# Four conditioning tiles on GpSimd, RMS chains placed anew, and a down product finished tile by tile

## The chip, the cores and the metric

The kernel runs on one core of a Trainium2 chip. The metric is the device time of one execution in microseconds (us). The engines are TensorE (PE; its weight loads are PEld), VectorE (DVE), ScalarE (ACT), GpSimd (POOL) and SyncE (SP, which here only issues DMAs). Each runs its instructions in order and waits on semaphores.

## The reference

One layer (DEPTH = 1) on 1024 tokens of width 1024: a Fourier mixer and a gated ConvFFN, each with an RMS norm in front and a gate behind, and a last RMS norm.

```python
m = jax.nn.silu(c) @ w_mod + b_mod                 # sh1, sc1, gt1, sh2, sc2, gt2
a = rms_norm(x, g_mix) * (1 + sc1) + sh1
f = jnp.fft.fft2(a.reshape(1, L, 4, 256), axes=(1, 3), norm="ortho").real
h = x + gt1 * (f.reshape(1, L, D) @ w_fnet_out)
a2 = rms_norm(h, g_ffn) * (1 + sc2) + sh2
g, v = jnp.split(a2 @ w_up, 2, axis=-1)            # 2 x 2816 columns
g = depthwise_conv3(g) + b_conv
h = h + gt2 * ((jax.nn.silu(g) * v) @ w_down)
return rms_norm(h, g_final)
```

## The kernel before

Activations lie transposed: 8 tiles (`dt`) of 128 features, with even tokens in columns 0 to 511 (block 0) and odd ones in 512 to 1023 (block 1). Most products run as three passes on operands split in a rounded high part ("h") and a remainder ("l").

**Conditioning.** The vector `m` has 6 sections. A section `s` is 8 tiles of `w_mod` (128x1024, `wm`), each multiplied with silu(c) and summed along its rows by one VectorE instruction (`mod_sum`, L145), with silu(c) in PSUM (`silp`). The tiles come over 7 buffers; SP loads tile k+7 when tile k has been used. Section 2 is the mixer's gate, 4 and 3 are scale and shift of the second norm.

**Step 2 of the Fourier transform** (L411 to L446) makes, for each of 4 groups `g`, three PSUM tiles `s2p`, `s2p`, `s2q`, from six banks that are used in turn. `split` (L402 ScalarE, L403 VectorE) turns them into `ph`, `pl`, `qh`, `ql`; `p1` (L421, L422) does it for one extra row. The functions `between[g]` put `w_lo` (L366, remainder of the output weights), `w_last` (L381, L382) and conditioning tiles between the groups on VectorE. GpSimd makes sums and differences of weights first (`w_prep`, L357, L358).

**`fnet_block`** (L533, L536) multiplies with the output weights: per block 8 tiles `dt`, 25 matmuls each (13 into `pw`, 12 into `qw`). ScalarE (L550, L551) and VectorE (L542) write the result to `ha`, GpSimd issues a DMA that adds `x` to it (L555); then ScalarE squares it (L471) and VectorE or GpSimd adds that to `sacc` (L476). `while_even` and `while_odd` run after each `dt`, `amid_odd` inside it.

**The RMS chain** of a block: `rstd_col` sums `sacc` over partitions on TensorE (`ssps`, L485), VectorE scales (L487), GpSimd takes the power -1/2 (L489); `rstd_diag` (L494) makes diagonals, and `rstd_row` broadcasts them by a matmul (`rb`, L499). `norm2` (L572, L573, L567) then makes the FFN's operands `a2`.

**FFN.** `plain` and `product` (L693) make the first three chunks of the up product, each from `op_hi` (L612) and `op_lo` (L616); the other 19 go through a Strassen-like scheme (X, Y, Z). The down product has 7 products of 11 steps into PSUM banks `dX`, `dY`; a step is 12 matmuls, three for each of four tiles `g` (L1091). Its end is the last norm of the odd half: add (L697), square (L1133), sum (`cols`, L1065), power, diagonal, broadcast, `last_norm` (L697), store (L1078).

Up to step 2 the order on PE, ACT and POOL is a scheduler's and that on DVE and SP the code's; from `fnet_block(0)` ACT and POOL follow the code too, and from `fnet_block(1)` PE does.

Of the kernel before, what the change touches and what calls it, by code (L numbers as in the profile page):

```python
# [30 lines left out]
KT = 8  # L31
# [13 lines left out]
def fourier_ffn_kernel(ctx: ExitStack, tc: tile.TileContext, xf, xs, xt, cb, wmod, vecs, cst, ml, sp, wfa, wfb, wfl, wup,  # L45
# [346 lines left out]
    mod_tiles(4, 0, 4)  # L392
# [35 lines left out]
    def gate_ffn():  # L428
# [90 lines left out]
    def fnet_block(blk, then, mid=lambda dt: None):  # L519
# [5 lines left out]
        for dt in range(KT):  # L525
# [3 lines left out]
            for ps, s, ah, al, m, c0 in ((pw, 1, ph, pl, n, pc), (qw, 0, qh, ql, 256, qc)):  # L529
# [51 lines left out]
    def while_even(dt):  # L581
# [11 lines left out]

    fnet_block(0, while_even)
# [41 lines left out]

    def while_odd(dt):
        if dt > 2:

            squares(1, dt - 3)  # L640
            spill(1, dt - 3)
            stat(1, dt - 3)
        if dt == 0:
# [4 lines left out]
        elif 1 < dt < 6:
            norm2(0, even[1], {2: (1, 2), 3: (3, 4), 4: (5, 6), 5: (7,)}[dt])
            if dt == 3:  # L650
                for n in ("A11", "A12", "A21", "A22"):
                    ops[0, n] = op_hi(part(0, n), f"op0{n}")
        if dt > 5:
            for n in (("A11", "A12"), ("A21", "A22"))[dt - 6]:
                op_lo(ops[0, n], part(0, n))

    def amid_odd(dt):

        if dt == 1:
            even.append(rstd_col(sacc[0], 512))  # L660
            tb.append(stage("tb"))
            rstd_diag(even[0], 512, tb[0][:, 512:])
        elif dt == 2:
            even.append(rstd_row(512, tb[0][:, 512:]))
# [4 lines left out]
    fnet_block(1, while_odd, amid_odd)  # L669
# [151 lines left out]
    for dt in (5, 6, 7):  # L821
        squares(1, dt)
        spill(1, dt)
        stat(1, dt)
# [28 lines left out]
    op_lo(ops[1, "A11"], part(1, "A11"))  # L853
    op_lo(ops[1, "A12"], part(1, "A12"))
# [205 lines left out]
    def cols(tiles):  # L1060

        ps = small("ssps")
        for n, t in enumerate(tiles):
            for j in range(4):
                nc.tensor.matmul(ps[:, j:j + 1], lhsT=t[:, j * P:(j + 1) * P], rhs=ones[:, 0:1],  # L1065
                                 start=(n == 0 and j == 0), stop=(n == len(tiles) - 1 and j == 3))
# [157 lines left out]
```

## Time and profile before

| | us |
|---|---|
| three runs: median (lowest to highest) | 825.66 (824.72 to 827.84) |
| the profiled execution's own time | 826.69 |
| its span, first to last instruction | 824.9 |
| PE busy | 778.9 |
| DVE busy | 606.7 |
| ACT busy | 344.4 |
| POOL busy | 128.2 |
| mean granted TensorE clock | 0.977 of full speed |

A busy share is a mean over stages with different limits, so it says little here. The tables by stretch show when TensorE waited and at which clock it ran; the waits say for whom.

### The profile page before, as it was taken

The page shows a single profiled execution, that of the slowest core. Times are in us where ns is not written, and L with a number is a line of the kernel's source. Part 1 is how long each engine was busy: PE and PEld are TensorE (multiplying, and loading weights), DVE is VectorE, ACT ScalarE, POOL GpSimd, SP SyncE. Part 2 cuts the span into 40 slices and gives each one's busy share as a digit, 9 for nine tenths or more (in the row PEclk, how much of TensorE's full clock was granted, in tenths as well). Part 3 has the DMA queues.
Part 4 walks back from the last instruction along what each step waited for, and adds up shares of the span by engine and source line. Part 5 has one row for each costly group of instructions (what it writes and reads, how often), then busy time and mean ns, then how long its engine had stood idle before and what let it go on. Part 6 is the DMA issues. An engine that isn't in the chain of part 4 may idle for free.

```text
span 824.9 us, 10510 instructions
## 1 busy us (share of the span) xinstructions
PE 778.9 (94%) x3588; PEld 633.3 (77%) x3588; DVE 606.7 (74%) x1001; ACT 344.4 (42%) x617; POOL 128.2 (16%) x168
## 2 busy tenths in 40 slices
PE   1998979799999999999999999999999999999994
PEld 0585978588888888888888888888888888888883
DVE  5998976697867777877777777776747766648573
ACT  7364425425623334343333334433544435345520
POOL 2053431100112121212121121212110000000000
PEclk9999989799999999999999999999999999999995
DMA  9999764702398777858597778676999765655532
GB/s 331 407 335 341 217 178 91 217 27 89 89 288 204 199 192 205 242 142 246 146 254 198 193 221 256 141 195 155 266 294 356 231 191 184 199 183 176 182 149 102
DMA packets 81959, 171.30 MB, mean 208 GB/s; under 512 B 9001, under 2 KB 13865, under 8 KB 81906
## 3 DMA queue, kind: packets, MB, share of 16 engines
q1 hardware_dynamic: 67218, 143.89, 49.6%
q0 software_dynamic: 14688, 26.75, 20.4%
q8 instruction: 28, 0.46, 0.2%
q14 instruction: 25, 0.20, 0.1%
HBM read 130.49 MB, written 51.64 MB: 221 GB/s over the span
## 4 chain that ended last, share of the span: by engine, by line
PE 82%; DVE 9%; DMA 3%; issue 2%; ACT 2%; POOL 1%; POOLq 0%; DVEq 0%; SPq 0%; ACTq 0%
PE Y L693 19%; PE dX L1091 15%; PE X L693 13%; PE Z L693 13%; PE dY L1091 11%; PE c L693 8%; DVE wm L145 2%; DMA ha<-in_xt 2%; DMA wm<-in_wmod 1%; DVE ha L542 1%; PE ssps L1065 1%; DVE ha L572 1%; DVE z L216 1%; PE s2p L441 1%; DVE w L216 1%
## 5 line engine op out<-in xcount | busy, mean ns | idle before, releaser
L616 DVE TENSOR_TENSOR dn<-wd,dn 128x512 fp32r<-128x512 f32 x154 | 99.9, 689 | 69.3 <-ACT dn L612 68.6
L612 ACT CAST dn<-wd 128x512 fp32r<-128x512 f32 x154 | 88.6, 618 | 99.8 <-PE dX L1091 41.5
L1091 PE MATMUL dX<-dn,dn 128*128 128x512 f32 x528 | 123.5, 394 | 0.0
L1091 PEld LDWEIGHTS dX<-dn,dn 128*128 128x128 f32 x528 | 99.1, 188 | 23.2 <-issue 0.5
L755 POOL DMA_DIRECT2D ha<-ha x44 | 38.9, 968 | 348.2 <-DVE ha L696 158.7
L1091 PE MATMUL dY<-dn,dn 128*128 128x512 f32 x396 | 92.1, 394 | 0.0
L1091 PEld LDWEIGHTS dY<-dn,dn 128*128 128x128 f32 x396 | 74.4, 188 | 17.2
L696 DVE TENSOR_TENSOR ha<-Y,ha 128x512 f32<-128x512 f32 x57 | 39.4, 690 | 25.6 <-PE Y L693 25.6
L979 ACT COPY ha<-X 128x512 f32<-128x512 f32 x19 | 11.1, 586 | 110.2 <-PE X L693 110.2
L742 ACT ACTIVATE ha<-ha 128x512 f32<-128x512 f32 x44 | 27.8, 632 | 57.2 <-DVE ha L697 57.2
L145 DVE CUSTOM_DVE_ANT_0 wm<-wm,silp 128x1024 f32<-128x1024 f32 x32 | 37.9, 1213 | 0.4 <-DMA wm<-in_wmod 0.2
L1069 POOL TENSOR_TENSOR r<-r,mhalf 128x4 f32<-128x4 f32 x2 | 2.0, 1020 | 200.6 <-DVE r L1068 200.6
L798 POOL DMA_DIRECT2D sg_s<-in_wdn x22 | 29.9, 1373 | 9.2 <-DMA sg_s<-in_wdn 9.2
L798 POOL DMA_DIRECT2D sg_s<-sg_s x22 | 27.5, 1258 | 16.8 <-DMA sg_s<-sg_s 9.8
L697 DVE SCALAR_TENSOR_TENSOR ha<-ha,vec 128x512 f32<-128x512 f32 (+1 forms) x38 | 28.6, 752 | 1.4
L697 DVE SCALAR_TENSOR_TENSOR ha<-X,vec,ha 128x512 f32<-128x512 f32 (+1 forms) x38 | 28.4, 746 | 0.7
L696 DVE TENSOR_TENSOR ha<-Z,ha 128x512 f32<-128x512 f32 x38 | 26.0, 685 | 1.2 <-PE Z L693 1.2
L166 PE MATMUL gr<-wm,sil 128*32 128x512 f32 x32 | 10.3, 771 | 15.2 <-ACT sil L256 15.1
L696 DVE TENSOR_TENSOR ha<-ha 128x512 f32<-128x512 f32 x33 | 22.4, 685 | 0.0
L771 ACT COPY ha<-ha 128x512 f32<-128x512 f32 x11 | 6.8, 621 | 33.7 <-DVE ha L697 33.7
L166 PEld LDWEIGHTS gr<-wm,sil 128*32 128x32 f32 x32 | 3.1, 131 | 23.0 <-issue 20.6
L555 POOL DMA_DIRECT2D ha<-in_xt x14 | 12.7, 927 | 43.4 <-DVE ha L542 37.5
(947 smaller groups left out, 2000.2 us busy)
## 6 DMA issues: line engine op xcount, KB each, us to landing
wm<-in_wmod SPq DMA_DIRECT2D x40, 512.0 KB, 7.5
ha<-ha POOLq DMA_DIRECT2D x44, 256.0 KB, 5.2
sg_s<-in_wdn SPq DMA_DIRECT2D x44, 256.0 KB, 6.0
wd<-sg_s SPq DMA_DIRECT2D x44, 256.0 KB, 2.7
us_u<-ha SPq DMA_DIRECT2D x33, 256.0 KB, 2.0
wd<-in_wdn SPq DMA_DIRECT2D x33, 256.0 KB, 3.1
wd<-us_u SPq DMA_DIRECT2D x33, 256.0 KB, 3.4
us_T<-ha SPq DMA_DIRECT2D x22, 256.0 KB, 5.2
```

The costliest lines, as they stand in the source:

```text
L145: nc.vector.tensor_tensor_reduce(out=t, in0=t, in1=silp, scale=1.0, scalar=0.0, op0=ALU.mult, op1=ALU.add, accum_out=mods[:, s, n:n + 1])
L166: nc.tensor.matmul(rows[x][32 * j:32 * j + 32, :], lhsT=sil32[:, 4 * q + j, :], rhs=tiles[j][:, 512 * x:512 * x + 512], start=(q == 0), st ...
L216: nc.vector.scalar_tensor_tensor(out=t, in0=xraw[4 * i + f + 1][:, cs_], scalar=rr[:, 4 * i + f + 1:4 * i + f + 2], in1=xraw[4 * i + f][:, ...
L612: nc.scalar.copy(out=t[:, HALF[0]], in_=src)
L616: eng.tensor_tensor(out=t[:, HALF[1]], in0=src, in1=t[:, HALF[0]].bitcast(F32), op=ALU.subtract)
L693: nc.tensor.matmul(ps, lhsT=lh, rhs=rh, start=(first and j == 0 and x == 0), stop=(last and j == 3 and x == 2), skip_group_check=more)
L696: tt = lambda out, a, b, op, eng=nc.vector: eng.tensor_tensor(out=out, in0=a, in1=b, op=op)
L697: stt = lambda out, a, s, b, op0, op1: nc.vector.scalar_tensor_tensor(out=out, in0=a, scalar=s, in1=b, op0=op0, op1=op1)
L742: nc.scalar.activation(out=u[c, blk], in_=u[c, blk], func=AF.Silu)
L755: nc.gpsimd.dma_start(out=t, in_=other, accum_op=ALU.add)
L798: nc.gpsimd.dma_start(out=sg[n][k], in_=sg[a][k] if a[0] == "s" else block(k, a), accum_op=ALU.add, max_dma_last_dim=2048)
L1091: nc.tensor.matmul(BANKS[i][g], lhsT=lh, rhs=rh, start=(i in FIRST and k == 0 and x == 0), stop=(k == K2 - 1 and x == 2), skip_group_check ...
```

## The change

1. Tiles (4,1), (4,3), (3,2) and (3,4) (section, tile) are multiplied on GpSimd (`mod_mul`) and summed on ScalarE (`mod_acc`). Tiles (3,6) and (3,7) stay on VectorE but move behind block 0's sum of squares, and take silu(c) from SBUF (`silc`).
2. Between the groups of step 2, the `p1` instructions go ahead of `w_lo`, and `w_lo` and tiles are dealt out anew.
3. The even RMS chain moves from `dt` 1 to `dt` 2 of block 1 and its broadcast to the end of that `dt`; the second norm's tiles come sooner and the odd squares later. The odd chain moves into `plain(1, 1, 1)`.
4. The down product's last three steps run tile by tile; two squares are added on VectorE and not summed by matmuls; diagonals are shared with ScalarE; features 6 and 7 get `g_final` beforehand and their last factor on GpSimd, from a copy of `rb`; the last four stores are single tiles.

```diff
+    def mod_mul(s, n):
+        t = w_tiles.pop((s, n))
+        nc.gpsimd.tensor_tensor(out=t, in0=t, in1=silc, op=ALU.mult)
+        return s, n, t
+    def mod_acc(s, n, t):
+        nc.scalar.activation(out=t, in_=t, func=AF.Copy, accum_out=mods[:, s, n:n + 1])
+        wm_ahead(1)
...
-    mod_tiles(4, 0, 4)
+    for n in (0, 2):
+        m = mod_mul(4, n + 1)
+        mod_tiles(4, n, n + 1)
+        mod_acc(*m)
...
-    w_lo(0, 1, 2, 3)
-    w_last(0)
     for ps, n, c0 in ((l0, 258, 0), (l1, 256, 258)):
...
+    w_lo(0, 1)
...
-    between = [lambda: (w_lo(4, 5), mod_tiles(4, 4, 5)), lambda: (w_lo(6, 7), w_last(1), mod_tiles(4, 5, 6)),
-               lambda: (gate1(), mod_tiles(4, 6, 8)),
-               lambda: (w_lo(8, 9, 10, 11), gate_ffn(), mod_tiles(3, 0, 1))]
+    between = [lambda: (w_lo(2, 3), w_last(0), w_lo(4)), lambda: (mod_tiles(4, 4, 5), w_lo(5, 6, 7), w_last(1)),
+               lambda: (gate1(), mod_tiles(4, 5, 7)),
+               lambda: (mod_tiles(4, 7, 8), w_lo(8, 9, 10, 11), gate_ffn(), mod_tiles(3, 0, 1))]
...
     def while_even(dt):
-        if dt:
-            mod_tiles(3, dt, dt + 1)
+        if dt in (1, 3):
+            later.append(mod_mul(3, dt + 1))
+        if dt in (1, 3, 4):
+            mod_tiles(3, {1: 1, 3: 3, 4: 5}[dt], {1: 2, 3: 4, 4: 6}[dt])
+        if dt in (2, 4):
+            mod_acc(*later.pop())
...
+    def amid_odd(dt):
+        if dt == 2:
+            even.append(rstd_col(sacc[0], 512, bank))
+            after_sil()
+            mod_tiles(3, 6, 7, silc)
+            tb.append(t_tile())
+            rstd_diag(even[0], 512, tb[0])
+            mod_tiles(3, 7, 8, silc)
...
+    def late_odd(dt):
+        if dt == 2:
+            even.append(rstd_row(512, tb[0]))
+            norm2(0, even[1], (0,))
...
-    plain(0, 2, 1, bank, lambda: C.update(rb=rstd_row(512, dg1)))
+    plain(0, 2, 1, bank)
...
+    plain(1, 1, 1, bank, {("1", 0): rms_odd, ("2", 1): lambda: C.update(rb=rstd_row(512, C["dg"]))})
...
+    n_step = 7 * K2 - 3
...
     for g in range(4):
+        for s in range(n_step, 7 * K2):
+            down_product(s, (g,), False, s == 7 * K2 - 1)
         hd = h2[:, g, HALF[1]]
         stt(hd, X[g], mods[:, 5, g:g + 1], hd, ALU.mult, ALU.add)
         nc.scalar.activation(out=sqs[g], in_=hd, func=AF.Square)
-    r1 = cols([accs[1]] + sqs)
+        if g < 2:
+            tt(accs[1], accs[1], sqs[g], ALU.add)
+    for t in (accs[1], sqs[2], sqs[3]):
+        cols(ssps[1], t, t is accs[1], t is sqs[3])
...
+    rbs = diags[0]
+    nc.scalar.copy(out=rbs, in_=rb[1])
+    for dt in (6, 7):
+        nc.gpsimd.tensor_tensor(out=h2[:, dt, HALF[1]], in0=h2[:, dt, HALF[1]], in1=rbs, op=ALU.mult)
+    for dt in range(6):
         last_norm(1, dt)
```

How it moves instructions, at three places. Line numbers of the changed kernel are its own; a row is line, operation, output<-inputs with their buffer numbers, and shape.

ScalarE, the end of the weights' casts and the first group of step 2, before:

```order
L421 CAST p1h0_671<-s2l0_612 128x258
L402 CAST ph0_595<-s2p0_0_677 128x258
L402 CAST ph0_595<-s2p1_0_678 128x256
L402 CAST qh0_603<-s2q_0_679 128x512
L402 CAST ph1_596<-s2p0_1_711 128x258
L421 CAST p1h258_674<-s2l1_613 128x256
```

and in the change:

```order
L432 CAST p1h0_640<-s2l0_614 128x258
L415 CAST ph0_597<-s2p0_0_660 128x258
L162 ACTIVATE wm41_566,mods_66<-wm41_566 128x1024
L415 CAST ph0_597<-s2p1_0_661 128x256
L432 CAST p1h258_643<-s2l1_615 128x256
L415 CAST qh0_605<-s2q_0_662 128x512
L162 ACTIVATE wm43_572,mods_66<-wm43_572 128x1024
L415 CAST ph1_598<-s2p0_1_703 128x258
```

The sums of the two GpSimd tiles (`wm41`, `wm43`) stand between the casts of step 2.

VectorE, from the last tile of block 0 to block 0's RMS chain, before:

```order
L542 SCALAR_TENSOR_TENSOR ha_797<-qw07_1093,mods_66,ha_797 128x255
L145 ISA wm37_807,mods_66<-wm37_807,silp_64 128x1024
L145 ISA mods_66 128x1
L476 TENSOR_TENSOR sacc0_828<-sacc0_828,sq_1124 128x512
L476 TENSOR_TENSOR sacc0_828<-sacc0_828,sq_1128 128x512
L542 SCALAR_TENSOR_TENSOR ha_797<-qw10_1156,ngt1_69,ha_797 128x256
L542 SCALAR_TENSOR_TENSOR ha_797<-qw10_1156,mods_66,ha_797 128x256
L142 TENSOR_TENSOR mods_66<-mods_66,vec_65 128x8
L487 TENSOR_SCALAR r_1216<-ssps_1211 128x4
L494 TENSOR_SCALAR tb_1219<-ident_74,r_1216 128x128 x4
```

and in the change:

```order
L559 SCALAR_TENSOR_TENSOR ha_796<-qw07_1092,mods_66,ha_796 128x255
L489 TENSOR_TENSOR sacc0_830<-sacc0_830,sq_1122 128x512
L489 TENSOR_TENSOR sacc0_830<-sacc0_830,sq_1126 128x512
L489 TENSOR_TENSOR sacc0_830<-sacc0_830,sq_1130 128x512
L559 SCALAR_TENSOR_TENSOR ha_796<-qw10_1158,ngt1_69,ha_796 128x256
L559 SCALAR_TENSOR_TENSOR ha_796<-qw10_1158,mods_66,ha_796 128x256
L559 SCALAR_TENSOR_TENSOR ha_796<-qw11_1190,ngt1_69,ha_796 128x256
L559 SCALAR_TENSOR_TENSOR ha_796<-qw11_1190,mods_66,ha_796 128x256
L503 TENSOR_SCALAR r_1241<-ssps_1236 128x4
L145 ISA wm36_800,mods_66<-wm36_800,silc_124 128x1024
L145 ISA mods_66 128x1
L510 TENSOR_SCALAR t_1249<-ident_74,r_1241 128x128 x4
```

No tile stands ahead of the three adds now; one stands between the scaling `r` and the diagonals.

TensorE, the last step and the sums of squares, before:

```order
L1091 MATMUL dX2_4828<-dn761_6483,dn760_6480 128x512 x3
L1091 MATMUL dX3_4829<-dn761_6483,dn760_6480 128x512 x3
L1065 MATMUL ssps_6542<-ones_70,acc1_4819 128x1 x4
L1065 MATMUL ssps_6542<-ones_70,sq0_4822 128x1 x4
L1065 MATMUL ssps_6542<-ones_70,sq1_4823 128x1 x4
L1065 MATMUL ssps_6542<-ones_70,sq2_4824 128x1 x4
L1065 MATMUL ssps_6542<-ones_70,sq3_4825 128x1 x4
L499 MATMUL rb_6570<-diag1_4821,ones_70 128x512
```

and in the change:

```order
L1120 MATMUL dX2_4832<-dn761_6489,dn760_6486 128x512 x3
L1120 MATMUL dX3_4833<-dn741_6437,dn740_6434 128x512 x3
L1120 MATMUL dX3_4833<-dn751_6467,dn750_6464 128x512 x3
L1120 MATMUL dX3_4833<-dn761_6489,dn760_6486 128x512 x3
L1089 MATMUL ssps1_6504<-ones_70,acc1_4823 128x1 x4
L1089 MATMUL ssps1_6504<-ones_70,sq2_4828 128x1 x4
L1089 MATMUL ssps1_6504<-ones_70,sq3_4829 128x1 x4
L515 MATMUL rb_6570<-diag1_4825,ones_70 128x512
```

A tile's nine matmuls (operands `dn74`, `dn75`, `dn76`) now follow each other, and 12 short sums stay of 20.

## Rows read from the trace of the kernel before

**Rows 1.** The page, TensorE's granted clock in 40 slices, in tenths.

```profile
PEclk9999989799999999999999999999999999999995
```

**Rows 2.** By stretch: length, busy us of five engines, PEclk, DMA share, GB/s.

```profile
66.40:82.55 16.15, 12.93 (x46) 8.43 (x46) 12.65 (x24) 5.87 (x15) 7.61 (x10) 0.89 0.94 322
82.55:112.25 29.70, 29.09 (x238) 28.69 (x238) 26.92 (x53) 11.95 (x26) 15.01 (x17) 1.00 0.75 196
117.36:125.36 8.00, 8.00 (x37) 7.52 (x38) 2.71 (x10) 0.00 (x0) 2.82 (x3) 0.59 0.66 183
147.90:162.70 14.80, 13.19 (x45) 10.18 (x46) 7.36 (x16) 3.96 (x7) 1.89 (x2) 0.77 0.75 224
162.70:215.00 52.30, 52.30 (x229) 42.50 (x228) 46.09 (x72) 23.82 (x39) 2.68 (x3) 1.00 0.25 74
```

**Rows 3.** What TensorE waited for, 60 to 165 us (total, times, longest).

```profile
PE ssps L485 <- DVE sacc L476: 6.7, 2, 5.1
PE c L693 <- DVE op0A L616: 4.7, 1, 4.7
PE s2p L441 <- DVE p L422: 2.5, 1, 2.5
PE pw L533 <- ACT qh L402: 0.7, 1, 0.7
PE c L693 <- ACT ha L551: 0.7, 1, 0.7
PE pw L533 <- DVE pl L403: 0.6, 1, 0.6
```

**Rows 4.** VectorE in order of time: start, us, line, operation [idle before].

```profile
62.74 1.22 DVE L145 CUSTOM_DVE_ANT_0 wm<-wm,silp 128x1024 f32<-128x1024 f32 x1
...
80.41 0.54 DVE L382 SCALAR_TENSOR_TENSOR wl<-wlh,vec,wlt 128x256 fp32r<-128x256 f32 x1 [3.06 <-ACT wlh L381]
...
101.50 2.13 DVE L366 TENSOR_TENSOR w3l<-u,w3h 128x512 fp32r<-128x512 f32 x1
...
107.02 0.46 DVE L542 SCALAR_TENSOR_TENSOR ha<-qw,mods,ha 128x255 f32<-128x255 f32 x1
...
125.38 0.75 DVE L572 SCALAR_TENSOR_TENSOR ha<-ha,G,rb 128x512 f32<-128x512 f32 x1 [2.41 <-PE rb L499]
...
147.16 1.29 DVE L616 TENSOR_TENSOR op0A<-wr0g,op0A 128x512 fp32r<-128x512 f32 x2
...
792.02 2.65 DVE L616 TENSOR_TENSOR dn<-wd,dn 128x512 fp32r<-128x512 f32 x4
...
794.59 5.35 DVE L697 SCALAR_TENSOR_TENSOR h<-h,vec,rb 128x512 f32<-128x512 f32 x8
```

**Rows 5.** GpSimd in order of time, and its short sums as a group.

```profile
101.45 1.62 POOL L476 TENSOR_TENSOR sacc<-sacc,sq 128x512 f32<-128x512 f32 x1
106.47 1.60 POOL L476 TENSOR_TENSOR sacc<-sacc,sq 128x512 f32<-128x512 f32 x1
111.19 1.28 POOL L476 TENSOR_TENSOR sacc<-sacc,sq 128x512 f32<-128x512 f32 x1 [0.95 <-ACT sq L471]
L357 POOL TENSOR_TENSOR u<-u 128x256 f32<-128x256 f32 x16 | 12.2, 771 | 15.5 <-DVE pl L403 15.4
```

**Rows 6.** ScalarE's 128x1024 sums of squares (group), and the chain's transfer for block 0.

```profile
L196 ACT ACTIVATE junk<-xr 128x1024 f32<-128x1024 f32 x6 | 6.3, 1051 | 0.3 <-DMA xr<-in_xf 0.2
92.81 5.79 DMA ha<-in_xt
```

**Rows 7.** The chain that ended last, its end: start, us, what.

```profile
804.65 6.40 PE ssps L1065 x40
813.36 2.09 PE rb L499 x2
```

**Rows 8.** The last stores: a stretch as in rows 2, and times to landing.

```profile
817.90:822.00 4.10, 0.00 (x0) 0.00 (x0) 3.00 (x5) 0.00 (x0) 0.00 (x0) 0.50 1.02 377
DMA to landing us min/median/max: 2.8/2.9/3.0
```

More of the change, by code (lines that the diff above doesn't have):

```diff
@@ L517, in squares, with fnet_block @@
         ssq[blk, dt] = square(sacc[blk], ha[:, dt, 512 * blk:512 * blk + 512], dt, 512, t2)
-    def fnet_block(blk, then, mid=lambda dt: None):
+    def fnet_block(blk, then, mid=lambda dt: None, late=lambda dt: None):
         n = 258 if blk == 0 else 256
@@ L537, in fnet_block @@
                     mid(dt)
+            late(dt)
             gp, gn = mods[:, 2, dt:dt + 1], ngt1[:, dt:dt + 1]
@@ L592, in while_even @@
             stat(0, d)
+    later = []
     fnet_block(0, while_even)
@@ L635, in part, with stats_odd @@
         return raws[c, "gv"[name[1] == "2"]][:, HALF[name[2] == "2"]]
-    def while_odd(dt):
[L638 to L643, printed above, removed]
+    def stats_odd(*dts):
+        for dt in dts:
+            squares(1, dt)
+            spill(1, dt)
+            stat(1, dt)
+    def while_odd(dt):
+        if 2 < dt < 6:
+            norm2(0, even[1], {3: (1, 2), 4: (3, 4, 5), 5: (6, 7)}[dt])
+        if dt == 5:
+            for n in ("A11", "A12", "A21", "A22"):
+                ops[0, n] = op_hi(part(0, n), f"op0{n}")
+            op_lo(ops[0, "A11"], part(0, "A11"))
+            op_lo(ops[0, "A12"], part(0, "A12"))
+        if dt > 5:
+            stats_odd(*{6: (0, 1, 2), 7: (3, 4)}[dt])
+        if dt == 7:
+            op_lo(ops[0, "A21"], part(0, "A21"))
+            op_lo(ops[0, "A22"], part(0, "A22"))
+    def amid_odd(dt):
[6 more added lines that the diff above has]
+            mod_tiles(3, 7, 8, silc)
             mod_bias(3, mods[:, 3, :])
-            after_sil()
             load_raw(0, "g")
             load_raw(0, "v")
[L648 to L664, printed above, removed]
+    def late_odd(dt):
+        if dt == 2:
+            even.append(rstd_row(512, tb[0]))
             norm2(0, even[1], (0,))
@@ L686, in fourier_ffn_kernel, with product @@
     te, to = ([ha[:, dt, o:o + 512] for dt in range(KT)] for o in (0, 512))
-    def product(t, b, ps, first, last, more=False):
+    def product(t, b, ps, first, last, more=False, amid={}):
         for j in range(4):
+            amid.get((b[1], j), lambda: None)()
             hi, lo = t[:, j * P:(j + 1) * P], t[:, 512 + j * P:512 + (j + 1) * P]
@@ L820, in fourier_ffn_kernel, with plain @@
     load_raw(1, "v")
[L821 to L824, printed above, removed]
+    stats_odd(5, 6, 7)
     C = {}
-    def plain(c, row, b, new, between=lambda: None):
+    def plain(c, row, b, new, amid={}):
         ps = C[c, row, b] = new(f"c{c}{row}{b}")
-        product(ops[c, f"A{row}1"], f"b1{b}", ps, True, False)
-        between()
-        product(ops[c, f"A{row}2"], f"b2{b}", ps, False, True)
+        product(ops[c, f"A{row}1"], f"b1{b}", ps, True, False, amid=amid)
+        product(ops[c, f"A{row}2"], f"b2{b}", ps, False, True, amid=amid)
     def gate_plain(c):
@@ L1058, in squares, with cols, rstd_of @@
         return one
[L1060 to L1066, printed above, removed]
+    def cols(ps, tile, first, last):
+        for j in range(4):
+            nc.tensor.matmul(ps[:, j:j + 1], lhsT=tile[:, j * P:(j + 1) * P], rhs=ones[:, 0:1], start=(first and j == 0),
+                             stop=(last and j == 3), skip_group_check=True)
+    def rstd_of(ps):
         r = tmp.tile([P, 4], F32, tag="r", bufs=2, name="r")
@@ L1083, in fourier_ffn_kernel, with down_product @@
     n_last = 6 * K2
-    for s in range(7 * K2):
+    ssps = {}
+    def down_product(s, gs, first, last):
         i, k = divmod(s, K2)
-        prepare(n_up + 2 * s + 2)
         at, bt = down[s, 0], down[s, 1]
-        for g in range(4):
+        for g in gs:
             hi, lo = at[:, g * P:(g + 1) * P], at[:, 512 + g * P:512 + (g + 1) * P]
@@ L1092, in fourier_ffn_kernel @@
                                  stop=(k == K2 - 1 and x == 2), skip_group_check=i not in FIRST)
+    n_step = 7 * K2 - 3
+    for s in range(n_step):
+        i, k = divmod(s, K2)
+        prepare(n_up + 2 * s + 2)
+        down_product(s, range(4), k == 0, k == K2 - 1)
         prepare(n_up + 2 * s + 8)
```

71 lines of the change are left out of this document (44 added, 27 removed).

## The prediction

> **What bounds the kernel now.** I read the page first: TensorE is busy 778.9 of 824.9 us, with a granted clock below 0.9 in slices 6, 8 and the last [rows 1]. So two places can pay: 66 to 163 us, where the Fourier mixer hands over to the FFN, and the end. The table by stretch gives the price of the first. TensorE's clock was 0.89, 0.59 and 0.77 of full in three stretches with 12.93, 8.00 and 13.19 us of matmuls [rows 2]; the lost share of each, 1.4, 3.3 and 3.0, makes **7.7 us**. The waits give the rest: 6.7, 4.7, 2.5, 0.7, 0.7 and 0.6 us, together **15.9 us** [rows 3]. The low clock follows the longer waits each time (2.5, 5.1, 4.7 and 1.6, which is the 6.7 without its longest). So 23.6 us are lost between 66 and 163 us; nearly all waits are for VectorE, which is busy 26.92 of 29.70 us in the stretch ahead of the 5.1 us wait [rows 2]. From 162.7 us on TensorE is busy without a gap [rows 2]. At the end 40 records of short sums (two for each) take 6.40 us, then come the power, the diagonals, a broadcast of 2.09 us at half clock, eight multiplies and the stores [rows 7].
>
> **The sum for the mixer.** I walk the changed queues with the durations of the rows, on the old time scale, and count what TensorE still loses.
>
> *Price of a GpSimd tile.* No 128x1024 multiply of two SBUF tensors is in the trace. From 128x256 (0.77) and 128x512 (1.28) the line gives 2.3 us; twice the usual 1.62 gives 3.2 [rows 5]. I take 2.8. The ScalarE sum I take as the 1.05 of the squares of that shape [rows 6]. VectorE is rid of two tiles of 1.22 us early (its row at 62.74 is tile (4,1)) and of four more ahead of block 0's chain; two of these come back behind it [rows 4]. The tile loads saturate the DMA there, so an early tile saved is in part a wait for the next one.
>
> *Step 2.* The wait of 2.5 us goes: the first `p1` multiply no longer stands behind five `w_lo` and `w_last`. The second stands behind ScalarE's sum of (4,1): 62.7 + 2.8 + 1.05 and two casts of 0.37 makes 67.4, and the bank it frees is needed at 68. With full clock step 2 ends some 4 us earlier, at 77.8. The next wait is late instead: VectorE's `w_last(1)` (which waited 3.06 us for ScalarE's cast before, until 80.41 [rows 4]) now waits for a cast queued behind `qh3`; cast at 78.9, `pl2` frees a bank at 79.5. So `fnet_block` starts at 79.5 and not at 82.6: TensorE loses **1.6**. It then catches VectorE's `pl3`, behind two tiles: **1.0** (0.6 before).
>
> *Block 0's chain.* TensorE reaches the sums after 263 matmuls now, at 29.09/238 = 0.122 us each: 79.5 + 1.0 + 32.1 = 112.6. The last addend is `dt` 5. GpSimd starts tile (3,4) near 100, behind the DMA of `dt` 3; 102.8, ScalarE's sum 103.9, a square and `pw05` 105.2, VectorE 106.0, the DMA lands 5.8 later [rows 6], square, two adds: 114.3. It was 117.4. TensorE waits **1.7**, not 5.1. From the sums to the broadcast TensorE had 25 matmuls as cover; now it has 12, 1.5 us, against sums 1.0, two evacuations that stand ahead of the scaling, scaling, power 1.0 and diagonals 0.9. GpSimd's power reads two SBUF tensors and starts beside tile (3,6), which now reads two as well: in the trace an instruction of 0.69 us took 2.13 beside GpSimd's 1.62 [rows 4, 5]. So I add half a tile: a wait of **2.0**, and the broadcast itself at half clock, 2.09 for 0.86: **1.0** more. It ends near 119.4, at a place 12 matmuls further on than at 125.4.
>
> The Trainium skill says why ("SBUF — State Buffer", section "Who interferes with whom"): VectorE with two SBUF inputs and a GpSimd read exclude each other for the whole instruction, and whichever issues first holds on. Our row at 101.50 agrees: VectorE ended one duration after GpSimd's end. By that rule alone the power waits for all of tile (3,6), 0.6 us more than I count, and the sum below is 12.8 and not 13.4.
>
> *To the first up product.* From broadcast to first `op0A` remainder VectorE took 22.4 us (125.38 to 147.8 [rows 4]), with one odd square's add and longer waits for ScalarE between. In the new order, eight norm tiles (1.32 each with the remainder), four evacuations of 0.8 and four ping-pong waits of 0.9 to 1.5 with ScalarE make 18.6: ready at 138.0. TensorE, with 125 matmuls (14.9) left, is there at 134.3: it loses **3.8**, where it lost 5.4. Such a wait cost clock before, so I add half of the 3.0: **1.5**.
>
> *Behind it.* The odd chain comes 27 matmuls of 0.23 us (6.3 us) later in TensorE's program, and its sums are ready at 149.8, before TensorE arrives: **0.2** left. VectorE's work behind that broadcast is then 6.3 us later against TensorE; it idled 6.2 of 52.3 us there [rows 2], mostly on casts that wait for TensorE. I count **0.9**.
>
> The losses left are 1.6 + 1.0 + 1.7 + 3.0 + 3.8 + 1.5 + 1.1 = 13.7: the mixer gains 23.6 - 13.7 = **9.9 us**.
>
> **The sum for the end.** The last three steps keep their 36 matmuls. Their operands must be ready 5 us sooner; VectorE made the last ones by 794.7 [rows 4] and the first tile starts at 795.9 (804.65 less 36 matmuls of 0.243), so this costs nothing. VectorE is busy with the even half's last norm until 799.9 [rows 4]; the first tile's add, square and sum follow while TensorE works, and the fourth tile's square is ready at 806.3. Then the last 8 of now 24 records are left, at 6.40/40 each about 1.3 us: 807.7, where the old end was 811.1: **3.4**. Half the diagonals on ScalarE save 0.2. The multiplies on GpSimd I count at nothing: from 817.9 on the stores move 377 GB/s at a DMA share of 1.02 [rows 8], and 2.1 MB at that rate last 5.6 us after the first pair, whoever made the rest. A smaller last store (2.9 us for 512 KB [rows 8]) gives at most 1. Bounds 2.5 and 4.6; I take **3.5**.
>
> Together 13.4 us: 826.69 - 13.4 = 813.3 for an execution like the profiled one, and the median of the runs is 1.0 lower: **812.3 us**. Some 4.1 us (0.5%) are what a measurement here can tell from no change.
>
> **The rivals.**
> - *The offload moves nothing.* GpSimd holds VectorE's `w_lo` 12 to 15, which stand beside tiles (3,2) and (3,4), for 2.8 us each, as the 2.13 us row did [rows 4], and ScalarE's evacuations wait behind both sums. Block 0's sum is then up to 5.6 us later: 7.8 us of gain, 817.9. For it: ScalarE's queue order. Against it: most of VectorE's work there reads PSUM, and such a row ran in 0.46 us beside GpSimd's 1.60 [rows 4, 5]. The Trainium skill's "Perfetto Trace Analysis", section "Optimizing Scalar/DVE Operations", warns of just this: work moved between the two engines may not help, as they share a read port. Chance 0.17.
> - *TensorE becomes the bound.* VectorE keeps up, the waits left are half of mine (7 us): 16.6 + 3.5 saved, 805.6. Chance 0.12.
> - *The gain is given back later.* The odd chain's 6.3 us are not absorbed: 5.4 more lost, 817.7. Against it: the idle 6.2 us [rows 2]. Chance 0.06.
> - *Slower.* Each GpSimd tile has an in-order queue behind it: (4,1) ScalarE's casts of step 2, (4,3) SP's loads of the next weights, (3,2) and (3,4) the evacuations. If GpSimd is starved between VectorE's instructions, each delays TensorE by its excess over 2.8. Four times the excess eats 13.4 us from 6.2 us per tile on; at 7.5 the time is 831. Against it: the same engine's 1.28 alone and 1.62 beside VectorE [rows 5], 1.3 times and not 2.2. Chance 0.04.
>
> **How the numbers follow.** The forecast has 0.61, with 808.5 to 816.5 as its own range. The range to 805 and 819.5 takes in the second, third and fourth case and the bounds of the tile's price (2.3 to 3.2, four times) and of the end. Of the cases near 818 a sixth or so lies above 821.5: faster 0.91, same 0.05, slower 0.04.
>
> **What would show it.** Right: GpSimd rows of 128x1024 near 2.8 us; the wait for `sacc` under 3 us and at a place behind `dt` 2; the wait for `op0A` still the largest, near 4; the granted clock in slices 4 to 8 nearer 1; 24 records of short sums at the end, and the last broadcast some 13 us earlier. Wrong: a new wait of `p1` or `qw` for ScalarE, GpSimd tiles over 4 us, VectorE's `w_lo` at 3 us, or TensorE gaps after the first up products.

## The result, and the profile after

The changed kernel takes **813.86 us** (median of 4 runs, 812.56 to 815.33) against 825.63 for the kernel before on the same chip (824.72 to 827.84): ratio 0.9847, 95% interval 0.982 to 0.9874. Its profiled execution took 812.85 us, span 811.1, mean granted clock 0.988 (before 0.977). In the experiments below one execution of `norm_dve` took 1985.52 us and is left out, so its median there is that of the other five.

What TensorE waited for from 60 to 170 us, in the changed kernel (total, times, longest), beside [rows 3]:

```profile
PE pw L549 <- DVE pl L416: 3.6, 1, 3.6
PE rb L515 <- DVE t L510: 1.7, 1, 1.7
PE c L725 <- ACT op0A L634: 1.6, 1, 1.6
PE c L725 <- DVE op0A L638: 1.0, 1, 1.0
PE qw L549 <- DVE ha L559: 0.7, 1, 0.7
PE c L725 <- DVE op1A L638: 0.4, 1, 0.4
```

The clock row of its page, as in [rows 1], and the stretches around its only low clock before the end, as in [rows 2]:

```profile
PEclk9999899999999999999999999999999999999996
```

```profile
80.00:84.00 4.00, 1.64 (x7) 1.67 (x8) 2.95 (x7) 2.31 (x6) 4.00 (x7) 0.66 0.94 308
84.00:88.00 4.00, 4.00 (x20) 4.00 (x20) 4.00 (x8) 1.11 (x2) 4.00 (x7) 0.50 0.53 147
88.00:110.00 22.00, 21.30 (x177) 21.09 (x176) 20.93 (x34) 11.23 (x25) 11.80 (x11) 1.00 0.74 196
110.00:125.00 15.00, 13.32 (x107) 12.64 (x106) 11.44 (x28) 5.23 (x11) 7.18 (x7) 1.00 0.84 221
125.00:165.00 40.00, 36.78 (x210) 31.07 (x209) 31.52 (x57) 20.81 (x39) 6.25 (x7) 1.00 0.60 168
```

The waits sum to 9.0 us. The low clock costs 1.64 x 0.34 + 4.00 x 0.50 = 2.6. So 11.6 of the 23.6 us lost before are lost still. The wait for `sacc` and the one for `p1` are gone; the wait at the first matmul of `fnet_block`, 0.7 before [rows 3], is 3.6, with the clock at its lower level (1.2 GHz) behind it. Behind 125 us, where 0.77 stood [rows 2], the clock stays at 2.4 GHz.

By these sums the mixer would gain 23.6 - 11.6 = 12.0 us. TensorE is 10.8 ahead at the last down matmul (below), and 1.0 of the difference stands ahead of all this: a matmul into `s2l` that starts at 62.00 us before starts at 62.99 here (61.97 to 63.30 in the runs below, so executions differ by that much).

TensorE, ScalarE, GpSimd and VectorE around that new wait, in order of time:

```profile
76.42 2.00 POOL L367 TENSOR_TENSOR u<-u 128x256 f32<-128x256 f32 x2 [7.34 <-DMA u<-in_wfb]
...
79.58 0.62 ACT L369 CAST w0h<-u 128x512 fp32r<-128x512 f32 x1 [2.13 <-POOL u L368]
...
80.10 0.58 ACT L415 CAST qh<-s2q 128x512 fp32r<-128x512 f32 x1
...
80.58 0.41 ACT L391 CAST wlh<-wlt 128x256 fp32r<-128x256 f32 x1
...
81.02 0.86 DVE L392 SCALAR_TENSOR_TENSOR wl<-wlh,vec,wlt 128x256 fp32r<-128x256 f32 x1 [2.06 <-ACT wlh L391]
...
81.80 0.74 DVE L416 TENSOR_TENSOR pl<-s2p,ph 128x258 fp32r<-128x258 f32 x2
...
82.36 0.55 PE L549 MATMUL pw<-ph,w0h 128*128 128x258 f32 x1 [3.61 <-DVE pl L416]
```

Read upwards: TensorE needs the bank that `pl` frees; `pl` stands behind `wl` on VectorE; `wl` behind two casts on ScalarE; those behind the cast of a weight unit, whose sums GpSimd began only when a transfer landed at 76.4. So the earlier step 2 does not bring the product forward: it starts at 82.36, and before it started here:

```profile
82.58 0.36 PE L533 MATMUL pw<-ph,w0h 128*128 128x258 f32 x1 [0.74 <-ACT qh L402]
```

What TensorE gains comes later. It is at block 0's sums at 117.53 us (117.36 before), but these now stand a whole `dt` (25 matmuls) further on in its program. It is 3.1 us ahead at the first up product (139.41; 142.47) and 10.8 at the last down matmul.

The end of the changed kernel, beside [rows 7]:

```profile
793.71 0.95 PE L1089 MATMUL ssps<-ones,acc 128*128 128x1 f32 x8
...
794.71 1.95 PE L1089 MATMUL ssps<-ones,sq 128*128 128x1 f32 x16
...
798.78 2.07 PE L515 MATMUL rb<-diag,ones 128*128 128x512 f32 x2 [2.13 <-ACT diag L1188]
...
800.89 0.59 ACT L1193 COPY diag<-rb 128x512 f32<-128x512 f32 x1 [2.16 <-PE rb L515]
...
801.51 0.75 DVE L729 SCALAR_TENSOR_TENSOR h<-h,vec,rb 128x512 f32<-128x512 f32 x1 [2.99 <-ACT diag L1193]
```

The 24 records of short sums take 3.0 us, not 6.4. The broadcast ends at 800.85 (before 815.45, 14.6 later), but the span ends only 13.8 earlier: VectorE's first multiply now waits for ScalarE's copy.

### The profile page after: what moved, and what is told of

It reads as the page before. It is cut to its first block, busy times and chain, and to the rows that moved or that the text cites. A ratio compares the mean times of both kernels' runs of the same rounds, so it can differ in the third digit from the quotient of the medians.

```text
span 811.1 us, 10498 instructions
## 1 busy us (share of the span) xinstructions
PE 770.4 (95%) x3572; PEld 625.5 (77%) x3572; DVE 606.0 (75%) x991; ACT 351.1 (43%) x630; POOL 140.6 (17%) x174
## 4 chain that ended last, share of the span: by engine, by line
PE 84%; DVE 5%; ACT 3%; DMA 3%; issue 2%; POOL 2%; SPq 0%; DVEq 0%; POOLq 0%; ACTq 0%
PE Y L725 19%; PE dX L1120 14%; PE X L725 13%; PE Z L725 13%; PE dY L1120 11%; PE c L725 7%; DVE h L729 1%; DMA xr<-in_xf 1%; PE po L305 1%; PE pw L549 1%; PE qw L549 1%; DVE wm L145 1%; DVE ha L589 1%; PE gr L176 1%; PE pe L317 1%
## 5 line engine op out<-in xcount | busy, mean ns | idle before, releaser
L145 DVE CUSTOM_DVE_ANT_0 wm<-wm,silp 128x1024 f32<-128x1024 f32 x26 | 30.8, 1214 | 1.9 <-DMA wm<-in_wmod 1.8
```

Source lines behind the costliest of these rows:

```text
L145: nc.vector.tensor_tensor_reduce(out=t, in0=t, in1=sil, scale=1.0, scalar=0.0, op0=ALU.mult, op1=ALU.add, accum_out=mods[:, s, n:n + 1])
```

## The experiments

Twelve runs, eleven of other kernels and one of the changed kernel again, each with five rounds beside the kernel before, on four chips (its medians there: 825.39 to 826.71). Medians in us:

| run | median | ratio to before, 95% |
|---|---|---|
| tail_only | 824.65 | 0.9984 (0.9962 to 1.0007) |
| mixer_only | 816.14 | 0.9878 (0.9849 to 0.9906) |
| no_offload | 813.76 | 0.985 (0.9822 to 0.9878) |
| wlast_late | 813.83 | 0.9852 (0.9824 to 0.9881) |
| step2_old | 817.24 | 0.9901 (0.9865 to 0.9936) |
| even_old | 816.55 | 0.9881 (0.9848 to 0.9915) |
| odd_old | 819.59 | 0.9925 (0.9896 to 0.9954) |
| norm_dve | 813.02 | 0.9842 (0.9806 to 0.9878) |
| after_again | 813.30 | 0.9838 (0.981 to 0.9866) |
| all_three | 812.90 | 0.9828 (0.98 to 0.9856) |
| all_three_b | 810.62 | 0.9803 (0.9776 to 0.983) |
| squares_late | **809.11** | 0.979 (0.9756 to 0.9823) |

### The two parts apart

`tail_only` is the kernel before with the new `cols`, `down_product` and the code behind them; `mixer_only` is the changed kernel with the old ones.

> The kernel before with the new end alone (the last three steps of the down product tile by tile, ScalarE's diagonals, GpSimd's final multiplies); the mixer is the old one. Theory (the two parts are independent, the end gives what its own chain gives): 3.0 us, of them 3.6 for the short sums less some 0.6 for the copy of the broadcast ahead of VectorE's first multiply; median 822.6, ratio 0.9964, and TensorE's waits between 60 and 163 us sum to 15 to 16 us as before. Rival (the end only pays because the mixer's gain shifts the operands or the stores): under 1 us, 825 or more.

> The changed kernel with the old end. Theory (independent parts): the mixer gives what TensorE is ahead by at the end of the down product, 10.8 us: median 814.9, ratio 0.987, with 40 records of short sums of 6.4 us at the end as before. Rival (part of the mixer's gain is given back between 160 and 790 us, and the end makes up for it): 816.5 or more.

The mixer alone gives 9.4 us, the end alone 0.9 (its interval takes in nothing and 3), on top of the mixer 2.3. That is less than the 3.0 that the two traces show from the start of the last down matmul to the end of the span (20.6 before, 17.6 after). A likely reason stands in the old end of `mixer_only`, TensorE's short sums:

```profile
795.94 0.95 PE L1091 MATMUL ssps<-ones,acc 128*128 128x1 f32 x8
...
796.75 3.71 PE L1091 MATMUL ssps<-ones,sq 128*128 128x1 f32 x32
```

The theories put the gains 2.0 and 1.2 us too high. The sums take 4.6 us there (795.9 to 800.5), at a granted clock of 1.00 in that stretch; in the profile of before the same 40 records took 6.4, at 0.67. Against 3.0 they save 1.6 in one execution and 3.4 in another. From the first short sum to the end of the span the old end lasts 20.4 us before and 18.4 in `mixer_only`, the new one 17.7 in `tail_only` and 17.4 in the changed kernel. So the new end is about as long with either mixer, against the rival of `tail_only`, and the end's size was read from an execution whose clock fell early. How often it falls early was not measured. The medians alone don't decide: 0.9 is under the rival's 1 us, and 0.9 + 9.4 = 10.3 agrees with 11.8 within the intervals. The rival of `mixer_only` falls: TensorE is 8.6 us ahead of before both at the first matmul into `X` (212.24; 220.79) and at the first short sum (795.94; 804.49), so nothing is given back between.

### The offload undone

```diff
-    for n in (0, 2):
-        m = mod_mul(4, n + 1)
-        mod_tiles(4, n, n + 1)
-        mod_acc(*m)
+    mod_tiles(4, 0, 4)
...
-        if dt in (1, 3):
-            later.append(mod_mul(3, dt + 1))
         if dt in (1, 3, 4):
-            mod_tiles(3, {1: 1, 3: 3, 4: 5}[dt], {1: 2, 3: 4, 4: 6}[dt])
-        if dt in (2, 4):
-            mod_acc(*later.pop())
+            mod_tiles(3, {1: 1, 3: 3, 4: 5}[dt], {1: 3, 3: 5, 4: 6}[dt])
```

> The changed kernel with the four tiles that GpSimd multiplies and ScalarE sums put back on VectorE in their place; chains, weights and the end stay as changed. Theory (the offload pays where VectorE is what TensorE waits for): two tiles of 1.22 us more ahead of the first casts of step 2, and two more ahead of block 0's sum, which would be ready at 119.2 where TensorE arrives at 117.5: 2.4 + 1.7 = 4.1 us slower than the changed kernel, median 818.0. Rival 1 (the places alone do it, the offload is worth nothing): 813.9. Rival 2 (the offload costs, since GpSimd holds VectorE's remainders for 2 to 4.5 us): 812 or less.

My theory fell: without the offload the time is the same (813.76 and 813.86, each to some 2.3 us by its interval). VectorE and GpSimd in the changed kernel:

```profile
65.43 1.22 DVE L145 CUSTOM_DVE_ANT_0 wm<-wm,silp 128x1024 f32<-128x1024 f32 x1 [1.31 <-DMA wm<-in_wmod]
...
96.28 2.28 DVE L376 TENSOR_TENSOR w0l<-u,w0h 128x512 fp32r<-128x512 f32 x1
...
101.97 4.48 DVE L376 TENSOR_TENSOR w3l<-u,w3h 128x512 fp32r<-128x512 f32 x1
...
114.52 2.30 DVE L489 TENSOR_TENSOR sacc<-sacc,sq 128x512 f32<-128x512 f32 x3 [1.07 <-POOL sacc L489]
```

```profile
94.92 3.07 POOL L158 TENSOR_TENSOR wm<-wm,silc 128x1024 f32<-128x1024 f32 x1
...
101.93 2.73 POOL L158 TENSOR_TENSOR wm<-wm,silc 128x1024 f32<-128x1024 f32 x1
104.28 1.61 POOL L489 TENSOR_TENSOR sacc<-sacc,sq 128x512 f32<-128x512 f32 x1
```

And VectorE in `no_offload`:

```profile
97.15 0.68 DVE L376 TENSOR_TENSOR w0l<-u,w0h 128x512 fp32r<-128x512 f32 x1
...
102.00 2.12 DVE L376 TENSOR_TENSOR w3l<-u,w3h 128x512 fp32r<-128x512 f32 x1
...
113.24 0.69 DVE L486 TENSOR_TENSOR sacc<-sacc,sq 128x512 f32<-128x512 f32 x1 [1.00 <-POOL sacc L486]
```

Early, VectorE waits 1.31 us for a load, as the prediction warned, and makes its first `p1` at 66.57 where `no_offload` does at 67.35: 0.8 us sooner for two tiles of 1.22 less. (Such a wait differs between executions: `all_three` below has 1.46 with all tiles on VectorE.) Late, it saves 2 x 1.22 = 2.4 us and pays 1.6 (2.28 for 0.68) and 2.4 (4.48 for 2.12), as the remainders are held by GpSimd's tiles. So its sums start 1.3 us sooner without the offload. `no_offload` loses as much again at the broadcast: a wait of 2.2 there (1.7 in the changed kernel), a clock of 0.59 behind it.

### The places undone, one at a time

In `step2_old`, `w_lo(0, 1, 2, 3); w_last(0)` stand ahead of the `p1` loop again and `between` is the old one. In `even_old`, tiles (3,6) and (3,7) are back in `while_even`, the sums behind `dt` 1's and the broadcast behind `dt` 2's `pw`. In `odd_old`, the odd squares, the `op_lo` and the odd chain are:

```diff
+        if dt > 2:
+            stats_odd(dt - 3)
...
+        if dt > 5:
+            for n in (("A11", "A12"), ("A21", "A22"))[dt - 6]:
+                op_lo(ops[0, n], part(0, n))
...
     plain(0, 1, 1, bank)
+    rms_odd()
-    plain(0, 2, 1, bank)
+    plain(0, 2, 1, bank, {("2", 0): lambda: C.update(rb=rstd_row(512, C["dg"]))})
```

> The changed kernel with step 2 as before: the four remainders w_lo 0 to 3 and w_last of 0 ahead of the two p1 multiplies, and the old split of w_lo, w_last and w_mod tiles between the groups; GpSimd's four tiles, both chains and the end stay as changed. Theory (step 2's new order only moved TensorE's wait from the p1 multiplies to the first FNet matmul, which started at 82.4 after the change and 82.6 before it): the wait for p1 comes back with 1 to 2.5 us, the one of 3.6 goes, the FNet product starts between 81.5 and 83, and the time is within 1 us of the changed kernel, 813 to 815. Rival (the early casts carry the gain, as the prediction had it): 2.5 us and their clock come back, 816.5 to 818.

> The changed kernel with block 0's RMS chain at its old place (sums behind odd dt 1's p product, broadcast behind dt 2's), the last two w_mod tiles ahead of it again and the norm spread over dt 2 to 5 as before. Theory (VectorE is full from 80 to 112 us in every version, so what TensorE waits for in front of the sums is the sum of VectorE's work; the place of the chain sets how much of it is ahead): two tiles of 1.2 us more ahead of the sum, which TensorE reaches 1.6 us sooner: it waits 3.5 to 4.5 us there, the broadcast is hidden, and some 2 us of clock go: 816.5 to 818.5, and the wait for the first up operands stays under 3 us. Rival (the chain's place only trades the wait for the sums against the wait for the broadcast): 813 to 815.

> The changed kernel with block 1's side as before: the odd squares from dt 3 on, the remainders of the first up operands at dt 6 and 7, and the odd RMS chain between the first two up products; step 2, block 0's chain, GpSimd's tiles and the end stay as changed. Theory (most of the mixer's gain comes from here: TensorE was 3.1 us ahead at the first up product and 10.8 at the end, so 7 to 8 us come between 142 and 165 us): the wait for the first up operand is 4 to 6 us again, the odd broadcast costs 1 to 2 with a low clock behind it, and 5 to 8 us come back: 819 to 822. Rival (the gain comes from block 0, which gives VectorE time for both orders): 814 to 815.5.

Each costs time: 3.4, 2.7 and 5.7 us against the changed kernel's 813.86. One TensorE wait of each kernel, in this order, shows where:

```profile
70.52 2.08 PE L455 MATMUL s2p<-ac,dg 128*128 128x256 f32 x4 [3.37 <-DVE p L435]
```

```profile
119.34 1.86 PE L501 MATMUL ssps<-ones,sacc 128*128 128x1 f32 x8 [3.27 <-DVE sacc L489]
```

```profile
PE c L723 <- DVE op0A L638: 5.9, 1, 5.9
```

In `step2_old` my theory fell and the rival held: the wait for `p1` is 3.4 us, longer than the 2.5 of before [rows 3], and the FNet product starts at 85.3. A part of that is the pairing with GpSimd, whose tile (4,3), 2.77 us from 66.35 on, held the last of the four remainders:

```profile
66.84 2.83 DVE L376 TENSOR_TENSOR w3l<-u,w3h 128x512 fp32r<-128x512 f32 x1
```

What the old order costs without GpSimd's tiles can be read from the kernel before and `tail_only`, which have it so: the product starts at 82.58 and 81.23 there, and at 82.36 and 81.21 in the two traces of the changed kernel. So the 3.4 us are what the old order costs beside GpSimd's tiles; that the new order is worth anything against the kernel before isn't shown. In `even_old` the theory held, its wait 0.2 short of the range. In `odd_old` it held but for the odd broadcast, which cost nothing. Block 1's side is the largest: the wait for the first remainder comes back (5.9; 4.7 before) with a clock of 0.85 from 142 to 165 us. The three and the end, each undone alone, sum to 14.1 us against 11.8 for the change: they may share some of it, and each figure is known to 2 or 3 us only.

### The new wait taken away

`wlast_late`:

```diff
-    lambda: (mod_tiles(4, 4, 5), w_lo(5, 6, 7), w_last(1)),
-               lambda: (gate1(), mod_tiles(4, 5, 7)),
-               lambda: (mod_tiles(4, 7, 8), w_lo(8, 9, 10, 11), ...
+    lambda: (mod_tiles(4, 4, 5), w_lo(5, 6, 7)),
+               lambda: gate1(),
+               lambda: (w_last(1), mod_tiles(4, 5, 8), w_lo(8, 9, 10, 11), ...
```

> The changed kernel with the second quarter of the last weight row (w_last of 1) taken from between groups 1 and 2 of step 2 to behind group 3, and the two w_mod tiles between groups 2 and 3 put behind it. Theory (TensorE's 3.6 us wait at the first matmul of the FNet product is VectorE standing for ScalarE's cast of that quarter, and the low clock behind it follows from the wait): the product starts near 79.4 and not at 82.4, the granted clock stays at 1.00 up to 95 us, and 5 to 6 us go: median 808.4. Half-way (the wait goes, the clock falls all the same): 811. Rival (the wait only moves, to the remainder of group 3 or to the first evacuations, which stand behind the same casts): 813 to 814.

The product starts at 79.9 and the clock stays at 1.00 to 96 us, as the theory said; the time is that of the rival. TensorE's longest wait (2.7 us, until 101.0) and the low clock (0.59 from 100 to 104 us) come 19 us later. ScalarE shows why:

```profile
98.59 1.06 ACT L162 ACTIVATE wm<-wm 128x1024 f32<-128x1024 f32 x1 [7.20 <-POOL wm L158]
```

```profile
PE pw L549 <- ACT ha L568: 2.7, 1, 2.7
```

ScalarE stands 7.2 us for GpSimd's tile (3,2), and `dt` 2's evacuation behind it in its queue. So the offload and this edit were tried together, with the copy at the end left out.

`norm_dve` alone first: no `rbs`, no GpSimd multiply; VectorE makes `dt` 6 and 7 with `tt(hd, hd, rb[1], ALU.mult)`.

> The changed kernel without the copy of the last broadcast and without GpSimd's two multiplies: VectorE makes all eight, the last two with one operand less, since ScalarE has scaled them already. Theory (the copy only delays VectorE's first multiply by 0.65 us, and the stores are the bound behind it, whoever multiplies): the first multiply starts within 0.1 us of the broadcast's end, and from the broadcast's end to the end of the span it takes 9.5 us instead of 10.2: 0.7 us faster in the trace, 813.2. Rival (GpSimd's two multiplies are on the path): VectorE's eighth ends 0.7 us later than the sixth now and the span with it, 814 to 814.6.

The broadcast and VectorE's first multiply there:

```profile
800.78 2.07 PE L515 MATMUL rb<-diag,ones 128*128 128x512 f32 x2 [2.13 <-ACT diag L1188]
802.90 4.04 DVE L729 SCALAR_TENSOR_TENSOR h<-h,vec,rb 128x512 f32<-128x512 f32 x6 [2.38 <-PE rb L515]
```

It starts 0.05 us behind the broadcast, not 0.66, and the span ends 9.25 us behind it (812.1 less 802.85) where it ended 10.25: the copy and GpSimd's two multiplies cost the end 1.0 us in the trace, and only 0.6 of it is the copy's delay. The other traces agree: 10.2 in `after_again`, 9.3 in `squares_late`, which has no copy. The medians (813.02 and 813.86) can't tell so little apart.

> The changed kernel as it is, on the chip of the next two runs, so that they have it beside them. Every theory: 813 to 814.5, with waits of 3.2 to 3.7 us at the first FNet matmul, 1.6 to 2.1 at block 0's broadcast and 1.6 plus 1.0 at the first up product.

> The changed kernel with three of the edits before together: the second quarter of the last weight row behind group 3, no tile on GpSimd and ScalarE, and all eight last multiplies on VectorE without the copy. Theory (in the run that only moved the quarter, TensorE's 2.7 us wait at 101 us is ScalarE, which stands 7.2 us for GpSimd's tile (3,2) with the evacuation of dt 2 behind it, and VectorE's remainders are held 2.6 and 4.5 us by the same tiles; without the tiles the early start is kept): the FNet product starts near 80, no wait over 1 us stands between 80 and 115, the clock stays at 1.00 there, ScalarE has no wait for GpSimd behind 93 us, and 3 to 4 us go, one of them at the end: 809.5 to 811. Rival (VectorE's own work between 80 and 115 us is the bound, 2.4 us of it more now): the wait goes to the sums of block 0 and the time is 812.5 to 814.

> The same three edits, and the first w_mod tile of group 3 ahead of the four remainders w_lo 8 to 11 instead of behind them. Theory (those remainders read two SBUF tensors and took 1.23 us each beside GpSimd's sums of the weight units, 0.68 when GpSimd was done; a w_mod tile takes 1.21 either way): two of the four fall behind GpSimd's last sum, 0.5 to 1 us of VectorE saved ahead of block 0's sums: up to 1 us faster than without it, 808.5 to 810.5. Rival (TensorE needs these remainders at dt 4 and they are late then, or the saving ends in VectorE's wait for ScalarE): same as without it, or up to 1 us slower.

`after_again` gave 813.30. `all_three` (812.90) is no faster than that by more than the runs spread, so its theory fell; the time is the rival's, but not its reason: the wait is not at the sums, but again at ScalarE's evacuation, 101 us, which now stands for a transfer:

```profile
PE qw L546 <- ACT ha L565: 2.8, 1, 2.8
```

```profile
94.76 1.99 POOL L569 DMA_DIRECT2D ha<-in_xt  x2 [3.42 <-DVE ha L556]
...
99.85 0.63 ACT L481 ACTIVATE sacc<-ha 128x512 f32<-128x512 f32 x1 [7.85 <-DMA ha<-in_xt]
```

VectorE finishes `dt` 0 behind four `w_lo`, GpSimd issues its transfer at 94.8, and ScalarE holds `dt` 2's evacuation behind the square of `dt` 0. A second loss stands earlier in the same trace, where this kernel's code is that of `no_offload`, whose trace has neither wait:

```profile
66.39 1.22 DVE L145 CUSTOM_DVE_ANT_0 wm<-wm,silp 128x1024 f32<-128x1024 f32 x1 [1.46 <-DMA wm<-in_wmod]
...
69.34 1.13 PE L451 MATMUL s2p<-ac,dg 128*128 128x256 f32 x4 [2.21 <-DVE p L430]
```

A tile's transfer came late, so `p1` did, and the granted clock was 0.57 from 70 to 74 us. The product started at 81.23, not near 80 as the theory had it.

`all_three_b` puts one tile ahead of those `w_lo`. Its last `w_lo` took 0.68 us and its first 0.86 where `all_three` had 1.23 and 1.30; it is 2.7 us faster than `after_again` on its chip, and no run of the one reaches the other (810.08 to 811.43; 812.69 to 814.93). Against `all_three` it is 2.3 us faster by medians, with ranges that just touch, where the theory allowed 1. In the traces it is 1.4 (809.0 and 810.4), and 0.5 of that is there when the product starts, ahead of the edit: its wait for `p1` was 1.9 us, with the clock at 1.00 behind it. The other 0.9 is of the theory's size. For the last of the wait at 101 us:

```diff
-        for d in {2: (0,), 3: (1,), 4: (2,), 5: (3,), 6: (4,), 7: (6, 5, 7)}.get(dt, ()):
+        for d in {3: (0,), 4: (1,), 5: (2,), 6: (3, 4), 7: (6, 5, 7)}.get(dt, ()):
```

> The best kernel so far (three edits and the w_mod tile ahead of the remainders), with block 0's squares one dt later on ScalarE (dt 0's behind dt 3's evacuation, and so on). Theory (TensorE's last wait of this stage, 2.5 us at 100 us with a clock of 0.62 behind it, is ScalarE standing 6.9 us for the transfer that adds dt 0's input, with the evacuation of dt 2 behind its square): the wait and the low clock go, TensorE is at block 0's sums 3 to 4 us sooner, but VectorE and GpSimd have them ready only 1 to 2 us sooner, so 1 to 2.5 us go: 808.5 to 809.5. Rival (the sums come later, since four additions now stand at the end of GpSimd's queue): 811 or more, with a wait at the sums.

TensorE's waits there, the largest five:

```profile
PE rb L512 <- DVE t L507: 2.2, 1, 2.2
PE c L718 <- ACT op0A L627: 1.6, 1, 1.6
PE qw L546 <- ACT ha L565: 1.0, 1, 1.0
PE c L718 <- DVE op0A L631: 1.0, 1, 1.0
PE c L718 <- DVE op1A L631: 0.4, 1, 0.4
```

The time is the theory's: 809.11 us (808.33 to 810.67), 17.6 less than before on its chip. The changed kernel was not run on that chip; its medians elsewhere are 813.86 and 813.30, and no run of either reaches one of these six. No tile is on GpSimd in it. The traces don't show that the squares did it. The first matmul of the product in `all_three_b` and in `squares_late`:

```profile
80.72 0.39 PE L546 MATMUL pw<-ph,w0h 128*128 128x258 f32 x1 [0.43 <-DVE pl L413]
```

```profile
77.84 0.39 PE L546 MATMUL pw<-ph,w0h 128*128 128x258 f32 x1 [0.19 <-DVE pl L413]
```

These 2.9 us are all of the difference between the two spans (809.0 and 806.2), and they stand ahead of the first square: no tile's transfer came late in this execution, and `p1` cost no wait. Behind that the edit does what the theory says, and loses it again. TensorE's wait at the evacuation falls from 2.5 to 1.0 us, the clock stays at 1.00 there, and TensorE is at block 0's sums 5.0 us sooner. Then the broadcast's wait is 2.2 and not 1.7, with a clock of 0.67 from 116 to 120 us, and at the first up product the lead is 2.8. By medians `squares_late` is 1.5 us below `all_three_b`, on another chip and with ranges that overlap, so what the edit is worth stays open.

## Why the prediction was right, point by point

**The forecast** was 812.3 us; it is 813.86. The mixer was to give 9.9: TensorE is 10.8 us ahead at the last down matmul (804.3 and 793.5), and `mixer_only` gives 9.4. The end was to give 3.5: 3.0 in the trace, 2.3 by medians. The sum is right, though several of its terms are not, and that is in part luck. Ahead of block 0's sums I counted 2.6 us of losses (1.6 and 1.0); the trace has 6.9 (3.6, a wait of 0.7 for `ha`, and 2.6 of clock). From the sums on I counted 11.1; the trace has 4.7. Errors of 4.3 and 6.4 us in opposite directions leave one of 2.1.

- *Price of a GpSimd tile*: 2.8 forecast; 2.36 twice, 3.07 and 2.73.
- *Step 2*: "cast at 78.9, `pl2` frees a bank at 79.5" failed. The cast ran at 80.58, the bank was free at 82.4: I had ScalarE's cast behind `qh3` only, and did not follow ScalarE's queue one row further up, to the weight unit that waits for GpSimd's sums and they for their transfer. Wait 3.6, not 1.6, and a clock of 0.66 and 0.50 behind it (2.6 us) that I did not count. The `p1` wait went as forecast, and `pl3` (1.0) did not come. So the 3.1 us that step 2 was to start the product sooner came to 0.2.
- *Block 0's chain*: sums 1.7 forecast, none measured, for the wrong reason: they were ready 2.5 us later than I said (116.8; the remainder held 4.48 us is in it), but TensorE, late by step 2, came at 117.5 and not at 112.6. The broadcast wait was sized right (2.0; 1.7), its half clock (1.0) did not come: it ran in 1.13 us, where the one at the end takes 2.07.
- *GpSimd's power* beside tile (3,6) took 1.48 us, where block 0's took 1.03 before: 0.45 more, where 0.56 of that tile was left when it issued. By the rule of the Trainium skill ("SBUF — State Buffer", "Who interferes with whom") it waits for all that is left; this trace agrees, and my half tile (0.6) came out near it.
- *First up product*: 3.8 plus 1.5 of clock; measured 1.6 + 1.0 and no clock. This is the largest term on the good side, and `odd_old` shows that block 1's order made it.
- *Behind it*: 1.1; 0.4 measured. No gain was given back: TensorE is dense behind 165 us.
- *The end*: the 24 records came as forecast. "The multiplies on GpSimd I count at nothing" failed: with their copy they cost 1.0 us. The 3.4 for the sums was the price at the low clock of one execution.
- *The signs named*: GpSimd's rows, `sacc`, the 24 records and the broadcast came as the signs of being right have it. The wait for `op0A` was not the largest (1.6 + 1.0 against 3.6 for `pl`), and one sign of wrong came, a `w_lo` of 4.48 us.

**The rivals.** "The offload moves nothing" was right in its mechanism, and wrong in its time: `no_offload` shows the offload worth nothing, with remainders held for 2.28 and 4.48 us where it said 2.8 each. But I had charged that against the whole gain, and the gain comes from the places, which the same change moved. For the two RMS chains with the work around them `even_old` and `odd_old` show it, 2.7 and 5.7 us; the 3.4 of `step2_old` hold only beside GpSimd's tiles. The sentence of the Trainium skill's "Perfetto Trace Analysis" ("Optimizing Scalar/DVE Operations"), that work moved between these two engines might not help, fits the run. The other three fell: TensorE still waits 9.0 us, nothing is given back, and no tile came near 6.2 us.

## What to carry to other kernels

When a change moves work to another engine and places it anew at once, run the two apart before you keep both: here the time was the same without the offload, and ahead of block 0's sums the engine that took the work held VectorE for longer (4.0 us) than it relieved it (2.4). Follow each in-order queue from the late instruction upwards until you stand at a transfer, since an edit that removes one wait hands it to the next instruction that stands in front of something late (`pl`, then the sum of a GpSimd tile, then a square). Price a tail at both clock levels if it is short TensorE work. Before you credit an edit with a difference between two traces, find where the lead begins: in `squares_late` it began ahead of the edit, with a transfer that came late in another execution of the same code.

## What the runs showed of the hardware

One VectorE instruction with two SBUF operands was held through two GpSimd instructions in a row: `w3l` was issued at 101.97, the tile ended at 104.66, GpSimd's next add followed from 104.28 to 105.89, and `w3l` ended at 106.45, 4.48 us for a row of 0.68 alone. In `wlast_late` the same row took 4.46 beside the same pair. Beside one add alone it took 2.12 (`no_offload`). Each time, as in the rows of 2.28 and 2.83 us above, it ended 0.55 to 0.57 us after the end of GpSimd's last multiply or add. I had expected it to come in between the two.

In the changed kernel the granted clock went to 0.50 behind the wait of 3.6 us, but stayed at 1.00 behind those of 1.7 and 1.6. Behind a wait of 2.2 for `p1` it was 0.57 (`all_three`), behind one of 1.9 at the same place 1.00 (`all_three_b`). Why it fell behind some of these and not behind others was not tried.
